# Handing out side steps at every second product of the heads' projections, with other estimates for the delta rule's steps

## The chip, the cores and the metric

The kernel runs on one core of a Trainium2 chip. The metric is the device time of one execution in microseconds (us). Three runs of the kernel before gave 2916.89, 2920.38 and 2922.33 us; their median, 2920.38 us, is the time that the change is measured against.

## What is computed

One inference step of a decoder layer (`DEPTH` is 1, width 2048) for a prompt of 512 tokens and a sample group of 8 sequences with 4 tokens each, all in fp32. Cut to what matters here:

```python
h = rmsnorm(x, norm_mix_g)
sq, sk, sv, gq, gk, gv, ga, gb, gz = split_cols(h @ w_in, IN_SPLITS)
o_sb  = stick_breaking_attention(q, k_all, v_all, ...)      # 8 heads x 128
o_gdn = gated_delta_rule(gdn_q, gdn_k, gdn_v, log_decay, beta, gdn_s0)   # 8 heads x 128
o_gdn = rmsnorm(o_gdn, gdn_out_norm_g) * silu(gz)
x = x + concat(o_sb, o_gdn) @ w_out
x = x + cross_attention(rmsnorm(x), mem_k, mem_v) @ w_xo    # 4 heads, 256 memory tokens
x = x + (silu(gate) * up) @ w_down                          # SwiGLU, hidden 5632
```

The gated delta rule works on chunks of tokens. For each chunk a unit lower triangular matrix (built from k.k, the decays and beta) is inverted, and then a state of 128 x 128 runs through the chunks one after the other: v_new = u - w state, o = q state + qk v_new, state = g state + k v_new.

## The kernel before, in words

**Dense work.** Every projection is made in products. One product (`products`, L212) multiplies one 128x128 block of a weight with 544 columns (512 of the prompt, 32 of the sample) of the activations. Weight and activation are both split into a high and a low part, and three of the four cross terms are computed, in two halves of 272 columns: six matmuls a product. A projection of 128 output columns (`project`, L225) is 16 products. Its weights are loaded from HBM in pieces of 512 KB (`weights`, L195) and split by ScalarE (L206) and VectorE (L207).

**Side work.** What the heads need beside that is written as Python generators: `sb_head` (stick-breaking, prompt), `sb_sample` (the same for the sample, over the paged cache), `gdn_head` (delta rule, prompt), `gdn_sample`. Each runs until its next `yield` and so is cut into steps of some matmuls and what VectorE (DVE), ScalarE (ACT) and GpSimd (POOL) do with their results. A step yields two numbers: an estimate of its length on TensorE (PE) in us, and a delay until its successor may be issued (1.5 when it is left out).

**The planner.** `Side` (L404) interleaves both at build time. It has a clock `now` and a `credit`. After each product `tick(0.68)` (L222, L455) adds 0.68 to the clock and 0.68 x `ratio` to the credit (at most 8), and while the credit is positive it takes a step whose successor delay has passed (`pick`), which adds the step's length to the clock and takes it from the credit. At most `limits` = (2, 1) generators run at a time: two heads, and one sample generator behind them. Before the projections of head n begin, `settle(n)` (L2299) forces the first four steps of head n-2 and whatever is left of head n-3, due or not (`finish`). The order of these calls sets the priority in which the framework's scheduler then arranges the instructions; it can still pass over one that it takes to be not ready. [...]

**The stages around the change** (kern, L2306 to L2359): projections and heads of the eight stick-breaking heads, the gates, projections and heads of the eight delta heads (`side.ratio` 0.65 over both), then eight gate projections (`gate_head`, ratio 2), then `drain`. The output projection, cross attention and the feed-forward part follow; the feed-forward part has an order written out by hand and no planner.

**A delta head's chain** (`gdn_head` L1045, `invert` L906): transposes of q, k, v; the decays (L1067 to L1076: exp on ACT, products on POOL); k.k and k.q (L1080, L1086), whose results DVE multiplies with what POOL made of the decays (L1083, L1088); a 16x16 inversion in small DVE operations through HBM (`invert16`); then two levels (16, 32) of each: four matmuls (L955) and a mask by DVE (L956), four matmuls (L960) and a subtraction by DVE (L962), four transposes (L919) and a copy by ACT (L921); a last level of two half-size products (L941, L946); then for each of four blocks: k.state (L1104) and DVE L1108, the inverse times that (L1111) with DVE L1112 and ACT L1113, and the new state and output (L1116, L1124, L1125) with DVE L1121 and L1127. At the end comes a norm (L1132) and the transposes of the output. The change touches the pairs that the steps from `invert`'s levels on yield.

Of the kernel before, what the change touches and what calls it, by code (L numbers as in the profile page):

```python
# [51 lines left out]
def bc(ap, shape):  # L52
    return ap.broadcast_to(shape)
# [202 lines left out]
class Stats:  # L256


    def __init__(self, c):
        self.c, self.seen = c, set()  # L260
        self.acc = c.tt("acc")
# [142 lines left out]
class Side:  # L404
# [4 lines left out]
    def __init__(self, c):  # L409
        self.c = c  # L410
        self.hi, self.lo, self.on = [], [], [[], []]
        self.now, self.credit, self.ratio, self.limits = 0.0, 0.0, 0.8, (2, 0)

    def put(self, g, low=False, tiles=None):

        e = [g, 0.0, tiles, 0]
        (self.lo if low else self.hi).append(e)
        return e
# [36 lines left out]
    def tick(self, dense):  # L455
        self.now += dense
        if not self.left():
            self.credit = 0.0
            return
        self.credit = min(self.credit + dense * self.ratio, 8.0)  # L460
        while self.credit > 0:
            e = self.pick()
            if e is None:
                break
            self.step(e)
# [402 lines left out]
def invert16(c, gt):  # L868

    nc = c.nc
    gt16 = c.tt("g16")
    g, t, prod = gt16[:32, 0:256], gt16[:32, 256:512], c.tt("p16")[:32]
    src, dst = c.scr[0], c.scr[1 + c.inv % 2]
    c.inv += 1

    def whole(x):
        return x.rearrange("(a x) -> a x", a=4)[:, : P * P].rearrange("a (j i) -> j a i", i=P)

    def blocks(x):
        return x.rearrange("(n x) -> n x", n=32)[:, : 16 * P].rearrange("n (r i) -> n r i", i=P)[:, :, :16]

    gv, tv = (x.rearrange("p (r i) -> p r i", r=16) for x in (g, t))
    nc.gpsimd.tensor_copy(t, c.id16)
    yield 0.0, 1.0
    nc.sync.dma_start(whole(src), v3(gt))
    yield 0.0, 2.5
    nc.sync.dma_start(gv, blocks(src))
    yield 0.0, 2.5  # L890
    nc.gpsimd.tensor_scalar(g, g, -1.0, None, ALU.mult)
    for i in range(1, 16):
        p3 = prod[:, : i * i].rearrange("p (n j) -> p n j", n=i)
        nc.vector.tensor_mul(p3, tv[:, :i, :i].rearrange("p j n -> p n j"), bc(gv[:, :i, i : i + 1].rearrange("p j o -> p o j"), [32, i, i]))
        nc.vector.tensor_reduce(tv[:, i, :i], p3, mybir.AxisListType.X, ALU.add)
        if i % 4 == 3:
            yield 0.0, 1.2 + i / 8
    nc.sync.dma_start(blocks(dst), tv)
    yield 0.0, 2.5
    tr = c.tt("T")  # L900
    nc.sync.dma_start(v3(tr), whole(dst))
    yield 0.0, 8
    return tr


def invert(c, gt, nc_, levels, res):  # L906

    nc = c.nc  # L910
    gv = v3(gt, nc_)

    def wide(m):
        return bc(m.rearrange("p (o i) -> p o i", o=1), [P, nc_, P])

    def transposed(x, n=P):
        ps = c.aux()
        for a in range(nc_):
            nc.tensor.transpose(ps[:n, a * n : (a + 1) * n], x[:n, a * P : a * P + n], c.ident[:n, :n])  # L919
        t = c.tt("TT")  # L920
        nc.scalar.copy(t[:n, : nc_ * n], ps[:n, : nc_ * n])  # L921
        return t

    if levels[0] == 16:
        tr = yield from invert16(c, gt)
        tt = transposed(tr)
    else:
        ps = transposes(c, gt, nc_)
        tr, tt = c.tt("T"), c.tt("TT")
        nc.vector.tensor_mul(v3(tr, nc_), v3(ps, nc_), wide(c.m1))  # L930
        nc.vector.tensor_sub(v3(tr, nc_), wide(c.ident), v3(tr, nc_))
        nc.gpsimd.tensor_mul(v3(tt, nc_), gv, wide(c.m1t))
        nc.gpsimd.tensor_sub(v3(tt, nc_), wide(c.ident), v3(tt, nc_))
    yield 0.12 * nc_
    for s in levels:
        if s == H:
            ttv = v3(tt, nc_)
            x = c.tt("X")
            ps = c.aux()
            for a in range(nc_):  # L940
                nc.tensor.matmul(ps[H:, a * H : (a + 1) * H], gv[:H, a, H:], tr[:H, a * H : (a + 1) * H], start=True, stop=True, tile_position=(0, H))  # L941
            nc.vector.tensor_copy(x[H:, : nc_ * H], ps[H:, : nc_ * H])
            yield 0.11 * nc_, .8
            ps = c.aux()
            for a in range(nc_):
                nc.tensor.matmul(ps[:H, a * H : (a + 1) * H], x[H:, a * H : (a + 1) * H], ttv[H:, a, H:], start=True, stop=True, tile_position=(H, 0))  # L946
            nc.vector.tensor_sub(ttv[:H, :, H:], ttv[:H, :, H:], ps[:H, : nc_ * H].rearrange("p (a i) -> p a i", a=nc_))
            yield 0.11 * nc_, .8
            continue
        trv, ttv = v3(tr, nc_), v3(tt, nc_)  # L950
        x = c.tt("X")
        xv = v3(x, nc_)
        ps = c.aux()
        for a in range(nc_):
            nc.tensor.matmul(ps[:, a * P : (a + 1) * P], gv[:, a, :], trv[:, a], start=True, stop=True)  # L955
        nc.vector.tensor_mul(xv, v3(ps, nc_), wide(c.lev[s]))  # L956
        yield 0.22 * nc_, 1.1
        ps = c.aux()
        for a in range(nc_):
            nc.tensor.matmul(ps[:, a * P : (a + 1) * P], xv[:, a, :], ttv[:, a], start=True, stop=True)  # L960
        second = [ap.rearrange("p c (q b s) -> p c q b s", b=2, s=s)[:, :, :, 1, :] for ap in (ttv, v3(ps, nc_))]
        nc.vector.tensor_sub(second[0], second[0], second[1])  # L962
        yield 0.22 * nc_, 1.7
        if s != levels[-1]:
            n = H if s * 2 == H else P
            tr = transposed(tt, n)
            yield 0.12 * nc_, 1.4
    res.append(tt)


def transposes(c, src, n=4, ps=None):
    ps = c.aux() if ps is None else ps
    for a in range(n):
        c.nc.tensor.transpose(ps[:, a * P : (a + 1) * P], src[:, a * P : (a + 1) * P], c.ident)  # L974
    return ps
# [12 lines left out]
def v3(t, n=4):  # L988
    return t[:, : n * P].rearrange("p (a d) -> p a d", a=n)
# [55 lines left out]
def gdn_head(c, h, qkv):  # L1045
# [17 lines left out]
    def at(x, a):  # L1063
        return x[:, a * 8 + h : a * 8 + h + 1]
# [32 lines left out]
    for a in range(4):  # L1097
        cols = slice(a * P, (a + 1) * P)
        ve = c.tt("ve")
        if st is None:  # L1100
            rr = vv[:, cols]
        else:
            ps = c.aux()
            nc.tensor.matmul(ps[:, :P], k[:, cols], st, start=True, stop=True)  # L1104
            rr = ve[:, 256:384]
            e = ve[:, 512:513]
            nc.vector.tensor_scalar(e, at(c.ecum, a), -1.0, None, ALU.mult)
            nc.vector.scalar_tensor_tensor(rr, ps[:, :P], e, vv[:, cols], ALU.mult, ALU.add)  # L1108
            yield 0.22, 1
        ps = c.aux()  # L1110
        nc.tensor.matmul(ps[:, :P], tt[:, cols], rr, start=True, stop=True)  # L1111
        nc.vector.tensor_scalar(ve[:, P : 2 * P], ps[:, :P], bke[:, a : a + 1], None, ALU.mult)  # L1112
        nc.scalar.activation(ve[:, :P], ps[:, :P], AF.Identity, scale=br[:, a : a + 1])  # L1113
        yield 0.22, 1.6
        pss = c.aux()
        nc.tensor.matmul(pss[:, :P], kn[:, cols], ve[:, P : 2 * P], start=True, stop=True)  # L1116
        new = c.pb.tile([P, P], F32, tag="st", name="st", bufs=3)
        if st is None:
            nc.vector.tensor_copy(new, pss[:, :P])
        else:  # L1120
            nc.vector.scalar_tensor_tensor(new, st, at(c.gend, a), pss[:, :P], ALU.mult, ALU.add)  # L1121
        pso = c.aux()
        if st is not None:
            nc.tensor.matmul(pso[:, :P], qd[:, cols], st, start=True, stop=False)  # L1124
        nc.tensor.matmul(pso[:, :P], dec[:, cols], ve[:, :P], start=st is None, stop=True)  # L1125
        nc.scalar.activation(ve[:, 384:512], pso[:, :P], AF.Square, accum_out=so[:, a : a + 1])
        nc.vector.tensor_copy(on[:, cols], pso[:, :P])  # L1127
        st = new
        yield 0.66, .9
    nc.sync.dma_start(c.o_gs_p[0, 0, h], st)  # L1130
    out_norm(c, f, so, 4)
    nc.vector.tensor_mul(v3(on), v3(on), col(f, 4))  # L1132
# [413 lines left out]
def cross(c, acts, st, x, side):  # L1546
# [2 lines left out]
    outs, heads = [], []  # L1549
    qs = c.pb.tile([P, 4, NS], F32, name="xqs")  # L1550
    ra = [lambda name, dt=dt, tag=tag: c.act.tile([P, T], dt, tag=tag, name=name, bufs=KD) for dt, tag in ((F32, "ah"), (F32R, "al"))]
    side.limits, side.ratio = (2, 1), 1.5
    for h in range(4):
        ps = project(c, c.w_xq, 0, h * P, acts)
        if h == 0:
# [686 lines left out]
def kern(ctx: ExitStack, tc: tile.TileContext, *args, stop=99):  # L2242
# [27 lines left out]
    side = c.side = Side(c)  # L2270
    with tc.tile_pool(name="pb", bufs=1) as pb:
# [31 lines left out]
            if n > 2:  # L2303
                side.finish(heads[n - 3])

        side.limits, side.ratio = (2, 1), 0.65  # L2306
        for h in range(8):
            settle(h)
            if h == 7:
# [35 lines left out]
                else:  # L2345
                    os[8 + h] = z

        side.ratio = 2
        for h in range(8):
            if h == 2:  # L2350
                settle(16)
# [67 lines left out]
```

## Time and profile before

| | us |
|---|---|
| median of three runs | 2920.38 |
| the profiled execution's own time | 2919.49 |
| its span, first to last instruction | 2917.8 |
| stick-breaking heads (from about 67 to 440 of the span) | 373 |
| delta heads (440 to 930) | 490 |
| gate projections (930 to 1083) | 153 |
| output projection to cross attention (1083 to 1560) | 477 |
| feed-forward part (1560 to the end) | 1358 |

The bounds of the stages are read from the evacuations of the projections (L401, L1016, L2228). The profile counts a matmul as busy from its start to its modelled end. One of 272 columns is listed with some 290 ns, but one starts every 125 ns: a PE that is listed as busy can still have lost time, and only the starts show it. PEclk is the clock that TensorE was granted, 1.00 being full speed.

### The profile page before, as it was taken

How to read it: one execution, taken by the hardware profiler on the slowest of the kernel's cores; microseconds unless marked ns; L12 is line 12 of the kernel's file. 1: busy time of each engine (PE TensorE's matmuls, PEld its weight loads, DVE VectorE, ACT ScalarE, POOL GpSimd, SP SyncE). 2: the span in 40 equal slices, each digit the busy share in tenths (PEclk: the TensorE clock that was granted, in tenths of full speed). 3: DMA queues.
4: the chain of work that ended last, by engine and by line, in shares of the span. 5: the costliest groups of instructions: out<-in, count | busy, mean ns of one | idle time of the engine just before them, and what ended most of it. 6: DMA issues, size and time to landing. Idle time of an engine off the chain costs nothing. (4 is left out here: it accounts for less than half of the span.)

```text
span 2917.8 us, 57065 instructions
## 1 busy us (share of the span) xinstructions
PE 2844.4 (97%) x22442; PEld 2726.1 (93%) x22442; DVE 2006.2 (69%) x3168; ACT 1447.2 (50%) x2760; POOL 718.9 (25%) x858
## 2 busy tenths in 40 slices
PE   8999999999999999999999999999999999999998
PEld 7998888888989989999789999999999999999998
DVE  5553434667676554537488888888888887888886
ACT  5445435534445354425654444444444446555675
POOL 3111112213112110003242334334333334221200
PEclk9999999999999999999999999999999999999999
DMA  7335443453342374442444555455455549866653
GB/s 223 99 89 160 141 137 119 125 172 90 91 136 83 109 219 147 146 121 91 160 141 139 160 171 166 149 166 164 149 154 172 153 137 267 264 207 190 195 170 96
DMA packets 632692, 442.71 MB, mean 152 GB/s; under 512 B 36107, under 2 KB 559704, under 8 KB 632424
## 3 DMA queue, kind: packets, MB, share of 16 engines
q1 hardware_dynamic: 600600, 384.64, 44.4%
q0 software_dynamic: 22176, 42.90, 4.7%
q10 hardware_dynamic: 9648, 11.54, 1.1%
q8 instruction: 176, 2.88, 0.4%
q14 instruction: 92, 0.75, 0.1%
HBM read 359.23 MB, written 79.75 MB: 150 GB/s over the span
## 5 line engine op out<-in xcount | busy, mean ns | idle before, releaser
L2044 PE MATMUL gu<-pr,wh 128*128 128x272 f32 x4944 | 673.2, 288 | 6.4 <-ACT pr L1673 2.7
L2044 PEld LDWEIGHTS gu<-pr,wh 128*128 128x128 f32 x4944 | 641.1, 189 | 8.0 <-ACT pr L1673 3.1
L218 PE MATMUL mm<-ah,wh 128*128 128x272 f32 (+1 forms) x2464 | 546.6, 302 | 5.8 <-ACT ah L334 3.5
L218 PE MATMUL mm<-al,wh 128*128 128x272 f32 (+1 forms) x2464 | 524.5, 292 | 0.7 <-DVE al L249 0.7
L218 PE MATMUL mm<-ah,wl 128*128 128x272 f32 (+1 forms) x2464 | 518.0, 291 | 0.1
L1924 PE MATMUL bank<-pr,wh 128*128 128x272 f32 x2464 | 466.1, 289 | 1.0 <-ACT bank L1952 1.0
L218 PEld LDWEIGHTS mm<-ah,wh 128*128 128x128 f32 (+1 forms) x2464 | 389.7, 189 | 33.7 <-issue 20.5
L207 DVE TENSOR_TENSOR wl<-wr,wh 128x512 fp32r<-128x512 f32 (+1 forms) x340 | 243.4, 719 | 230.6 <-ACT wh L206 219.7
L218 PEld LDWEIGHTS mm<-al,wh 128*128 128x128 f32 (+1 forms) x2464 | 391.4, 189 | 3.7 <-DVE al L249 0.9
L218 PEld LDWEIGHTS mm<-ah,wl 128*128 128x128 f32 (+1 forms) x2464 | 388.0, 189 | 2.4 <-issue 0.8
L1924 PEld LDWEIGHTS bank<-pr,wh 128*128 128x128 f32 x2464 | 385.6, 188 | 2.9 <-ACT bank L1952 2.7
L206 ACT CAST wh<-wr 128x512 fp32r<-128x512 f32 (+1 forms) x340 | 208.2, 615 | 314.1 <-PE mm L218 267.2
L2044 PE MATMUL gu<-pr,wl 128*128 128x272 f32 x2472 | 361.8, 289 | 1.9 <-issue 1.8
L1924 PE MATMUL bank<-pr,wl 128*128 128x272 f32 x1232 | 354.1, 287 | 0.0
L2044 PEld LDWEIGHTS gu<-pr,wl 128*128 128x128 f32 x2472 | 330.5, 189 | 2.3 <-issue 1.9
L1822 DVE TENSOR_TENSOR wl<-sum,wh 128x1024 fp32r<-128x1024 f32 x172 | 219.6, 1277 | 76.5 <-ACT wh L1818 76.5
L1924 PEld LDWEIGHTS bank<-pr,wl 128*128 128x128 f32 x1232 | 231.9, 188 | 0.0
L1818 ACT CAST wh<-sum 128x1024 fp32r<-128x1024 f32 x172 | 180.3, 1049 | 77.4 <-PE gu L2044 42.8
L1822 DVE TENSOR_TENSOR wl<-raw,wh 128x1024 fp32r<-128x1024 f32 x133 | 202.9, 1527 | 15.3 <-ACT wh L1818 13.4
L1818 ACT CAST wh<-raw 128x1024 fp32r<-128x1024 f32 x133 | 139.8, 1051 | 102.3 <-PE gu L2044 95.0
L2109 POOL DMA_DIRECT2D pr<-hT x154 | 81.9, 548 | 254.2 <-PE bank L1924 227.7
L1811 DVE TENSOR_TENSOR sum<-raw,sum 128x1024 f32<-128x1024 f32 x86 | 136.0, 1582 | 0.7
(530 smaller groups left out, 4153.0 us busy)
## 6 DMA issues: line engine op xcount, KB each, us to landing
raw<-in_w_gate_up SPq DMA_DIRECT2D x176, 512.0 KB
wr<-in_w_in SPq DMA_DIRECT2D x108, 512.0 KB
raw<-in_w_down SPq DMA_DIRECT2D x176, 256.0 KB
hT<-hs SPq DMA_DIRECT2D x154, 272.0 KB
pr<-hT POOLq DMA_DIRECT2D x154, 272.0 KB, 6.6
page<-in_cache_sb_k SPq DMA_DIRECT2D x128, 128.0 KB
page<-in_cache_sb_v SPq DMA_DIRECT2D x64, 256.0 KB
wr<-in_w_out SPq DMA_DIRECT2D x32, 512.0 KB
```

Source lines behind the costliest of these rows:

```text
L206: nc.scalar.copy(hi[:, :m, :n], raw[:, k : k + m, :n])
L207: nc.vector.tensor_sub(lo[:, :m, :n], raw[:, k : k + m, :n], hi[:, :m, :n].bitcast(F32))
L218: c.nc.tensor.matmul(ps[:n, h, :HT], l[:, :n], r[:, h * HT : (h + 1) * HT], start=first and i == 0, stop=last and i == 2,)
L1811: self.f.c.nc.vector.tensor_sub(self.a[q], self.a[x], self.a[y])
L1818: self.f.c.nc.scalar.copy(self.hi[q], self.left(q))
L1822: self.f.c.nc.vector.tensor_sub(self.lo[q], self.left(q), self.hi[q].bitcast(F32))
L1924: self.c.nc.tensor.matmul(self.c.bank[bank][:, o], t[x][:, s, i * P : (i + 1) * P], pairs[i].op[q][r], start=new and not (i or n), stop=se ...
L2044: self.c.nc.tensor.matmul(bank, w[:, i * P : (i + 1) * P], self.pairs[i].op[q][r], start=start and n == 0, stop=n == 23, skip_group_check= ...
L2109: self.c.nc.gpsimd.dma_start(t, self.hT[2 * g + pair, :, max(0, 2 * n - 1) + k])
```

## The change

The planner can be told to hand out steps only at every second product (`every`), and is told so in the two stages of the heads; the ratio there goes from 0.65 to 0.75. From the gate projections on it is again every product. In the delta rule the estimated lengths go down to about 55% (0.22 to 0.12 for a group, 0.66 to 0.36 for the state step), and the delays become 1.1 to 1.5 where they were 0.8 to 1.7. No instruction is added or taken away.

```diff
@@ class Side, __init__
         self.now, self.credit, self.ratio, self.limits = 0.0, 0.0, 0.8, (2, 0)
+        self.every, self.ticks = 1, 0
@@ class Side, tick
         self.credit = min(self.credit + dense * self.ratio, 8.0)
+
+        self.ticks += 1
+        if self.ticks % self.every:
+            return
         while self.credit > 0:
@@ invert, level 64: L943 and L948
-            yield 0.11 * nc_, .8
+            yield 0.06 * nc_, 1.2
...
-            yield 0.11 * nc_, .8
+            yield 0.06 * nc_, 1.2
@@ invert, levels 16 and 32 (and 2): L957, L963, L967
-        yield 0.22 * nc_, 1.1
+        yield 0.12 * nc_, 1.5
...
-        yield 0.22 * nc_, 1.7
+        yield 0.12 * nc_, 1.5
...
-            yield 0.12 * nc_, 1.4
+            yield 0.12 * nc_, 1.5
@@ gdn_head: L1109, L1114, L1129
-            yield 0.22, 1
+            yield 0.12, 1.2
...
-        yield 0.22, 1.6
+        yield 0.12, 1.5
...
-        yield 0.66, .9
+        yield 0.36, 1.1
@@ cross, L1552
-    side.limits, side.ratio = (2, 1), 1.5
+    side.limits, side.ratio, side.every = (2, 1), 1.5, 1
@@ kern, before the heads, L2306
-        side.limits, side.ratio = (2, 1), 0.65
+        side.limits, side.ratio, side.every = (2, 1), 0.75, 2
@@ kern, before the gate projections, L2348
-        side.ratio = 2
+        side.ratio, side.every = 2, 1
```

## Prediction

> **What bounds the kernel now.** I read the page's first part, then busy time by stage, then the waits of TensorE, then the timeline of the longest waits.
>
> ```profile
> PE 2844.4 (97%) x22442; PEld 2726.1 (93%) x22442; DVE 2006.2 (69%) x3168; ACT 1447.2 (50%) x2760; POOL 718.9 (25%) x858
> ...
> core 0: us, PE busy (x) PEld busy (x) DVE busy (x) ACT busy (x) POOL busy (x), PEclk, DMA share, GB/s
> ...
> 67.00:440.00 373.00, 368.74 (x2897) 329.76 (x2897) 166.10 (x287) 170.44 (x378) 65.95 (x118) 1.00 0.42 126
> 440.00:930.00 490.00, 469.90 (x3748) 427.49 (x3747) 318.04 (x813) 231.50 (x614) 102.59 (x168) 0.98 0.41 118
> 930.00:1083.00 153.00, 146.37 (x1115) 138.16 (x1114) 85.20 (x219) 64.88 (x163) 33.95 (x47) 0.97 0.48 140
> ...
> 67.00:1083.00 1016.00, 985.00 (x7756) 895.41 (x7756) 569.34 (x1318) 466.81 (x1154) 202.49 (x333) 0.98 0.42 124
> ```
>
> PE bounds the kernel: 2844.4 of 2917.8 us. The change only reorders, and only in the three stages from 67 to 1083. There PE is not busy for 1016.0 - 985.0 = 31.0 us (4.3 with the stick-breaking heads, 20.1 with the delta heads, 6.6 in the gate projections), and the granted clock is 0.98 and 0.97 in the last two: 490 x 0.02 + 153 x 0.03 = 14.4 us of full-speed time withheld. Waits and slow clock together, 45 us, bound what an order can give. The order can't make a matmul cheaper:
>
> ```profile
> 799.64 0.38 PE L1116 MATMUL aux<-ve,kn 128*128 128x128 f32 x2
> 799.86 0.39 PE L1124 MATMUL aux<-st,qd 128*128 128x128 f32 x2
> 800.09 0.39 PE L1125 MATMUL aux<-ve,cumrow 128*128 128x128 f32 x2
> 800.23 0.50 PE L218 MATMUL mm<-ah,wh 128*128 128x272 f32 x2
> 800.56 0.41 PE L218 MATMUL mm<-al,wh 128*128 128x272 f32 x2
> 800.81 0.41 PE L218 MATMUL mm<-ah,wl 128*128 128x272 f32 x2
> ```
>
> Columns: start, length, engine and line. Starts are 0.25 us apart for two dense matmuls, so a product takes 0.75 us; they are 0.22 us apart for one side matmul of 128x128 (two records). So the old estimate, 0.22 a matmul, is the true length, and the new one is half of it. The planner's clock will run slow after delta steps; their new delays are therefore longer in truth than they read. From 799.64 to 800.56 six side records and two dense matmuls take 0.92 = 6 x 0.112 + 0.25: going into side work and out of it costs nothing.
>
> ```profile
> PE aux L960 <- DVE X L956: 6.2, 2, 4.5
> PE aux L715 <- ACT kT L704: 4.9, 4, 2.7
> PE aux L715 <- POOL win L686: 4.1, 2, 2.8
> PE aux L919 <- DVE TT L962: 3.9, 2, 3.3
> PE aux L1111 <- DVE ve L1108: 3.1, 3, 1.3
> ...
> DVE gt L1083 <- POOL gt L1082: 15.9, 7, 5.5
> ```
>
> Columns: sum in us, times, longest. Most of the loss lies in few events, and these are side steps that were issued before their operand was there. The longest:
>
> ```profile
> 703.90 0.29 PE L218 MATMUL mm<-ah,wh 128*128 128x272 f32 x1
> 708.73 1.98 PE L960 MATMUL aux<-TT,X 128*128 128x128 f32 x8 [4.54 <-DVE X L956]
> ...
> 706.27 0.69 DVE L1083 TENSOR_TENSOR gt<-gt,aux 128x512 f32<-128x512 f32 x1 [5.45 <-POOL gt L1082]
> 707.38 0.69 DVE L1088 TENSOR_TENSOR cumrow<-cumrow,aux 128x512 f32<-128x512 f32 x1 [0.43 <-POOL cumrow L1087]
> 707.99 0.68 DVE L956 TENSOR_TENSOR X<-aux,lev 128x512 f32<-128x512 f32 x1
> ...
> 708.00:711.00 3.00, 2.27 (x11) 2.28 (x12) 1.53 (x4) 0.00 (x0) 2.61 (x6) 0.64 0.40 95
> 711.00:714.00 3.00, 3.00 (x20) 2.46 (x19) 0.16 (x1) 0.48 (x2) 1.00 (x3) 0.79 0.01 0
> ```
>
> One head's gt product (L1083) stands on DVE waiting for POOL; the other head's mask (L956) is queued behind it, and PE behind that, with every dense product behind PE. After 4.54 us of idleness the clock is 0.64 and 0.79 for 6 us, which costs 3 x 0.36 + 3 x 0.21 = 1.7 us more.
>
> **What the change does to the order.** I worked the planner's bookkeeping through, call by call, with the yields of the code. Before, 12 of the 16 products L960 of the prompt's heads come at most one product (0.75 us) after their L955; after, 3 of 16, the rest two or more. The transposes L919 go the other way: from 1 of 16 at no or one product to 5 of 16 in the same slot as L960 (a long step of another generator carries the clock past the delay). L1111 behind L1104 stays at two products, 21 of 24 before and 20 of 24 after. The page steps of the samples (0.6, delay 0.4) were one product apart in 59 of 80 cases and become two apart in 69. The same number of steps falls into 273 slots where it fell into 338; slots with four steps or more go from 6 to 15. A delay of 1.5 is longer than two products (1.36), so a head that nothing else overtakes waits for four.
>
> **The cost, part by part**, in PE time of these stages.
>
> L956 to L960: 6.2 us in 2 waits. What L960 needs is DVE's 0.68 us plus its queue. One product more covers a plain queue, not the wait for POOL, because the spacing from the decay step to L1083's step is already two or more products in six of eight heads and is exactly two after. I take half: -3.1, and half of the 1.7 us of slow clock: -0.9. Bounds: -7.9 and 0.
>
> L962 to L919: 3.9 us in 2 waits. Five pairs in one slot now need DVE's 0.42 us covered by the other generator's matmuls, 0.9 us and more each (eight records of 0.112). I take +1.0. Bounds: -3.9, and +2.1 (5 x 0.42).
>
> L1108 to L1111, 3.1 us: same spacing, 0. Bounds -3.1 and +3.1.
>
> L715, 5.9 us of the 9.0 in these stages (the rest is in cross attention):
>
> ```profile
> L715 PE MATMUL aux<-kT,win 128*32 128x128 f32 x512 | 28.1, 289 | 5.9 <-POOL win L686 4.1 <-ACT kT L704 1.8
> ```
>
> The row is of 67 to 1083. POOL's 4.1 is the start of a sample, a queue on POOL that a step of distance doesn't clear; the copies by ACT (1.8) get a product more, of which I take -1.3. Bounds: -5.9 and 0.
>
> The states of the first delta sample (L1212):
>
> ```profile
> 749.50 5.14 PE L1212 MATMUL aux<-sqk,s 128*128 128x8 f32 x40
> 754.50 0.57 PE L218 MATMUL mm<-ah,wh 128*128 128x272 f32 x1
> ...
> 754.00:757.00 3.00, 3.00 (x15) 3.00 (x15) 0.00 (x0) 0.62 (x1) 0.00 (x0) 0.50 0.54 162
> 757.00:760.00 3.00, 3.00 (x16) 3.00 (x15) 1.11 (x2) 1.21 (x2) 0.00 (x0) 0.50 0.00 0
> ```
>
> Five steps of 8-column matmuls run in one block though the planner had them a product apart, and the clock stands at 0.50 for the 6 us behind it, 3.0 us lost, though PE was busy throughout. After, they are two to four products apart. I take -2.2, bounds -3.0 and 0.
>
> Settling. Before, head 4's last two steps were forced, three products after its L1125. After, heads 1, 2 and 3 are forced; for 1 and 2 the transposes still come six products after L1125, for head 3 two (1.5 us).
>
> ```profile
> 873.74 0.39 PE L1125 MATMUL aux<-ve,cumrow 128*128 128x128 f32 x2
> ...
> 875.73 0.69 DVE L1132 TENSOR_TENSOR on<-on,sm 128x512 f32<-128x512 f32 x1
> ...
> 983.53 0.39 PE L1125 MATMUL aux<-ve,cumrow 128*128 128x128 f32 x2
> ...
> 986.80 0.69 DVE L1132 TENSOR_TENSOR on<-on,sm 128x512 f32<-128x512 f32 x1
> ```
>
> From L1125 to the end of the norm are 2.7 and 4.0 us, so PE could wait 1.2 to 2.5 us once, less what the scheduler puts in between. I take +1.0, bounds 0 and +2.5.
>
> Fuller slots: nine more with four steps or more. Not shown by a row of its own; nearest is the block above. I take +0.5; from above it is rival A.
>
> The rest of the 31.0 us is 31.0 - 6.2 - 3.9 - 3.1 - 5.9 = 11.9 us, single waits of a microsecond or so of many kinds. All spacings but the zeros grow from one or two products to two: I take a sixth, -2.0. A new order also draws new collisions: bounds -6 and +6.
>
> Nothing is late at the end:
>
> ```profile
> L1136 ACT ACTIVATE o<-aux,gains x8: 669/688/689, 625.0 to 1044.3; 128x512 f32<-128x512 f32 x8
> L401 DVE TENSOR_TENSOR gz<-mm,rstd x8: 712/724/725, 955.8 to 1081.9; 128x544 f32<-128x544 f32 x8
> ```
>
> The last head's output (L1136) starts 37.6 us before the last gate projection is evacuated. By the bookkeeping the last side step moves from product 884 to 895 of 912, 8 us later; the cover of three gate projections shrinks to one, and costs nothing while it is there. No DMA is moved past a dense weight load except the pages and states, on SP's queue with the weights; their rate over a stage is unchanged.
>
> Sum: -3.1 - 0.9 + 1.0 - 1.3 - 2.2 + 1.0 + 0.5 - 2.0 = -7.0 us. The profiled execution took 2919.49 us, 0.9 below the median of the three: 2919.5 - 7.0 = 2912.5 us.
>
> **Rivals.**
>
> A, slower: the clock gate decides. Slots of four and more steps put matmuls with few rows or columns side by side, and the rows at 754 show that the clock falls behind such a block with no idleness at all, by 3.0 us each time. If four of the nine new full slots do that and the sum's gains halve (-3.5), the kernel is 12 - 3.5 = 8.5 us slower: 2928. It decides from two such blocks on. For it: the rows at 754. Against it: most full slots hold 128x128 matmuls of heads, and the run of six at 799.64 left the next dense pair at 0.25 us. [...]
>
> B, no difference: the scheduler passes over what it takes to be unready, so the planner's distance matters little, and what remains (DVE behind POOL at L1083, 15.9 us in 7 waits, up to 5.5) depends on engines that the change doesn't touch. Then only the redrawing of the 12 us is left, within 5: 2919.5, or 2915 to 2924. For it: the spacing of the decay step to L1083's is hardly changed. Against it: L960's is.
>
> C, faster by more: PE saves at the borders of side runs, of which there are 338 - 273 = 65 fewer. The second dense pair behind a side run starts 0.33 us after the first, 0.08 more than in a stream; were that a cost, 65 x 0.08 = 5.2 us more would go: 2907. Against it is the sum 0.92 above: the first pair starts early by as much. [...]
>
> **How the numbers follow.** The forecast has 0.45, A 0.17, B 0.30, C 0.08. The predicted time is 2912.5. The bounds of the forecast's terms, taken together as independent, reach about 7 to 8 us to either side: 2905 to 2920. The range takes in C and most of A: 2900 to 2928. About 0.2% (5.8 us) is what a measurement of this kernel can tell from no change. Faster by more than that: C and a good part of the forecast, and a little of B: 0.50. Within it: the rest of the forecast and most of B: 0.33. Slower: A: 0.17.
>
> **What would show it.** Right: PE's idle time from 67 to about 1075 falls below 27 us and PEclk of the delta stage is 0.99; the row L960 <- X L956 falls by half; L1212 no longer stands in one block of 40. Wrong in a step: a wait of L919 or of the output's transposes above 2 us; PEclk of 0.97 or less with the delta heads (A); rows of L1083 and L956 with the same long waits (B). Work moved past 1083, or a changed time of the feed-forward part, would make the whole account wrong.

## The result, and the profile after

The changed kernel takes 2891.46 us (median of four runs, 2891.30 to 2892.98), the kernel before, beside it, 2920.18 us (2916.89 to 2922.33). The ratio is 0.9902 [0.9888, 0.9916]: 28.7 us faster. 2912.5 was predicted, and 2900 to 2928 as the range: the sign was right, the size a quarter of what came. The profiled execution took 2891.30 us, its span is 2889.6.

Lines behind L464 carry a number 5 higher in the changed kernel (L956 is L961, L960 L965, L1082 L1087, L1083 L1088, L1212 L1217). The first part of its page, busy time by engine:

```profile
PE 2821.6 (98%) x22442; PEld 2713.2 (94%) x22442; DVE 2015.0 (70%) x3168; ACT 1446.6 (50%) x2760; POOL 728.8 (25%) x858
```

Its busy time by stage; the rows are the stick-breaking heads, the delta heads, the gate projections, and the three together:

```profile
core 0: us, PE busy (x) PEld busy (x) DVE busy (x) ACT busy (x) POOL busy (x), PEclk, DMA share, GB/s
53.00:435.00 382.00, 377.80 (x2980) 340.81 (x2980) 168.08 (x296) 171.63 (x381) 70.14 (x120) 1.00 0.42 125
435.00:908.00 473.00, 457.77 (x3749) 421.11 (x3749) 321.56 (x808) 230.61 (x609) 107.65 (x168) 0.99 0.42 123
908.00:1050.00 142.00, 139.80 (x1123) 133.88 (x1122) 90.59 (x224) 66.36 (x168) 35.23 (x47) 1.00 0.52 152
53.00:1050.00 997.00, 975.37 (x7847) 895.80 (x7848) 580.24 (x1327) 468.59 (x1157) 213.02 (x335) 1.00 0.44 128
```

The delta heads are 17 us shorter, the gates 11, the stick-breaking heads, whose own pairs are unchanged, 4. PE's idle time over the three is 997.0 - 975.4 = 21.6 us where it was 31.0, and the clock is 0.99 and 1.00 where it was 0.98 and 0.97. TensorE's waits, and DVE's wait for POOL, of the changed kernel (sum in us, times, longest):

```profile
PE aux L720 <- ACT kT L709: 5.2, 4, 2.7
PE aux L1116 <- DVE ve L1113: 3.7, 5, 1.5
PE aux L924 <- DVE TT L967: 2.7, 2, 1.9
PE aux L924 <- DMA T<-scr: 2.6, 1, 2.6
...
PE aux L965 <- DVE X L961: 1.0, 2, 0.8
...
DVE gt L1088 <- POOL gt L1087: 10.0, 6, 2.2
```

L965 waits 1.0 us where it waited 6.2. The row of L720 (L715) for POOL's win, 4.1 us before, is gone altogether. DVE's longest wait for POOL has gone from 5.5 to 2.2 us.

**One account for all kernels.** To compare the kernels I take the three stages together, from the evacuation of the first projections to that of the last gate projection, and split their time in three: PE's idle time as listed; the time in which the trace has the granted clock at about half, which costs up to half of its length (two dense matmuls start 0.45 us apart at 880 us of the changed kernel, at half clock, and 0.25 us apart at 885, at full clock); and the rest. Before: 1027.7 = 31.3 idle + 30.7 / 2 + 981.0. After: 996.7 = 21.8 + 6.8 / 2 + 971.5. So of the 31.0 us that the stages lost, 9.5 are idle time, 12.0 clock, and 9.5 appear in neither: over that time PE is listed as busy, and no run here shows where it went. Ahead of the stages 1.2 us go as well, and behind them, where nothing was changed, 4.1 come back (1835.8 to 1839.9): 28.1 us, against 28.2 between the two profiled executions. That unchanged code takes 1834.7 to 1839.2 us in fifteen of the sixteen other kernels and 1843.0 in q1, so the 4.1 are about the spread of single executions.

| kernel | steps at every n-th product | median us | ratio to before | three stages | idle | half clock | rest |
|---|---|---|---|---|---|---|---|
| before | 1 | 2920.2 | | 1027.7 | 31.3 | 30.7 | 981.0 |
| after | 2 | 2891.5 | .9902 [.9888, .9916] | 996.7 | 21.8 | 6.8 | 971.5 |
| e1: slots and ratio | 2 | 2887.5 | .9892 [.9872, .9911] | 995.8 | 18.9 | 3.4 | 975.2 |
| e2: estimates | 1 | 2903.5 | .9945 [.9927, .9963] | 1008.2 | 26.2 | 6.8 | 978.6 |
| e3: ratio | 1 | 2908.9 | .9962 [.9948, .9975] | 1016.0 | 28.1 | 20.4 | 977.7 |
| e4: after, old ratio | 2 | 2890.4 | .9897 [.9875, .9919] | 997.4 | 16.3 | 6.8 | 977.7 |
| m1: least delay | 1 | 2903.1 | .9930 [.9906, .9955] | 1010.7 | 28.1 | 13.6 | 975.8 |
| m2: delays | 1 | 2908.1 | .9953 [.9936, .9971] | 1016.9 | 32.0 | 17.0 | 976.4 |
| m3: lengths | 1 | 2902.1 | .9934 [.9906, .9962] | 1010.7 | 25.3 | 13.7 | 978.6 |
| m4: e1, every third | 3 | 2904.0 | .9934 [.9910, .9958] | 1008.6 | 22.8 | 20.5 | 975.6 |
| p1: before, POOL early | 1 | 2895.2 | .9914 [.9897, .9930] | 1002.4 | 20.1 | 6.8 | 978.9 |
| p2: after, POOL early | 2 | 2889.1 | .9887 [.9870, .9903] | 1001.7 | 20.2 | 17.1 | 973.0 |
| q1: before, sample later | 1 | 2899.7 | .9936 [.9916, .9955] | 1001.1 | 22.1 | 0 | 979.0 |
| q2: after, sample back | 2 | 2890.2 | .9903 [.9876, .9930] | 997.0 | 22.3 | 3.4 | 973.0 |
| r1: ratio 0.70 | 1 | 2904.8 | .9947 [.9927, .9967] | 1012.8 | 28.1 | 20.5 | 974.5 |
| s1: e1, sample later | 2 | 2893.7 | .9913 [.9896, .9931] | 998.0 | 20.8 | 3.4 | 975.5 |
| s3: e2, sample later | 1 | 2904.9 | .9953 [.9936, .9971] | 1009.5 | 24.8 | 10.2 | 979.6 |
| s4: p2, states apart | 2 | 2889.3 | .9892 [.9875, .9908] | 997.6 | 21.8 | 6.8 | 972.4 |

The medians are of two to five runs (before: seven to ten beside each group), which lie within 7 us of each other, but for q1 (9 us) and q2 (14 us, three runs at 2887 to 2890 and one at 2901). The last four columns are of one execution. The rest hardly moves (971 to 981), while idle time plus half of the half-clock time goes from 19.7 to 46.7: what these orders change is mostly waits and clock.

### The profile page after: what moved, and what is told of

Its sections match the earlier page's. It is cut to its first block, busy times and chain, and to the rows that moved or that the text cites. A ratio compares the mean times of both kernels' runs of the same rounds, so it can differ in the third digit from the quotient of the medians.

```text
span 2889.6 us, 57077 instructions
## 1 busy us (share of the span) xinstructions
PE 2821.6 (98%) x22442; PEld 2713.2 (94%) x22442; DVE 2015.0 (70%) x3168; ACT 1446.6 (50%) x2760; POOL 728.8 (25%) x858
## 5 line engine op out<-in xcount | busy, mean ns | idle before, releaser
L1827 DVE TENSOR_TENSOR wl<-raw,wh 128x1024 fp32r<-128x1024 f32 x133 | 203.5, 1531 | 15.2 <-ACT wh L1823 13.7
```

What stands on the lines that cost most here:

```text
L1827: self.f.c.nc.vector.tensor_sub(self.lo[q], self.left(q), self.hi[q].bitcast(F32))
```

## The experiments

The theories in the expectations are: D, the distance of two products clears waits; E, the new estimates do; L, luck, that is, any new order would do about as well; B, steps handed out in pairs save PE time at the borders of side runs; P, a collision on POOL's queue makes the long waits.

**Which part does it.** Four kernels: the old pairs with every second product and ratio 0.75 (e1); the new pairs alone (e2); the ratio alone (e3); the whole change with the old ratio (e4).

```diff
e2  -  side.limits, side.ratio, side.every = (2, 1), 0.75, 2
    +  side.limits, side.ratio, side.every = (2, 1), 0.65, 1
e3  -  side.limits, side.ratio = (2, 1), 0.65
    +  side.limits, side.ratio = (2, 1), 0.75
e4  -  side.limits, side.ratio, side.every = (2, 1), 0.75, 2
    +  side.limits, side.ratio, side.every = (2, 1), 0.65, 2
```

> The old lengths and delays of the delta rule, handed out at every second product with ratio 0.75. Theory D (distance: two products between the steps of a chain, and with it fewer waits and fewer spells of half clock, which comes from handing out at every second product): most of the gain of the heads' stages, 2898 to 2904 us, the delta stage near 473 us, the gate stage (every product in both kernels) still near 152 us. Theory E (the new lengths and delays do it): within 5 us of 2920. Theory L (luck: any other order draws its collisions anew, and the kernel before had drawn badly): anything from 2890 to 2925, with no relation between stage and edit.

> The new lengths and delays alone, every product, ratio 0.65. Theory D: 2908 to 2915 us, the delta stage within 6 us of before (489), only the gate stage near 142 us. Theory E: 2895 us or less. Theory L: anything from 2890 to 2925.

> Ratio 0.75 alone, all else as before. Theories D and E: 2917 to 2925 us, since neither distance nor estimates change; half clock in the heads' stages as long as before (some 30 us). Theory L: off 2920 by more than 6 us in either direction.

> The changed kernel with the ratio back at 0.65. Theories D and E: 2888 to 2897 us, as the ratio only sets how soon work is handed out. Theory L: 2890 to 2920, by chance near neither.

Measured: 2887.5, 2903.5, 2908.9 and 2890.4 us. e1 is 10 us below the range of theory D, e2 lies between those of D and E, and e3, for which both expected no change, is 11 us faster, as only L allowed; e4 came as D and E expected. Handing out at every second product, with the new ratio, gives the whole gain without the new estimates, and somewhat more than the whole change, though the two intervals overlap. The estimates alone give 16.6 us, the ratio alone 11.3; on top of the slots (the steps at every second product) each is about nothing. The slots with the old ratio and the old estimates were not run. The parts don't add up: they remove in part the same losses, or, as L has it, any of them only leaves an unlucky order. The estimates alone leave the long wait where it was. From the timeline of e2, one row of DVE and one of PE (start, length, engine, line, idle time before):

```profile
705.58 0.69 DVE L1088 TENSOR_TENSOR gt<-gt,aux 128x512 f32<-128x512 f32 x1 [3.93 <-POOL gt L1087]
...
707.98 0.63 PE L924 MATMUL aux<-ident,TT 64*64 64x64 f32 x4 [3.61 <-DVE TT L967]
```

And the busy time of e2 in the two stretches of 3 us there (columns as in the stages above, the granted clock third from the end):

```profile
706.00:709.00 3.00, 1.02 (x6) 0.85 (x7) 1.29 (x3) 0.35 (x1) 2.73 (x7) 0.61 0.31 87
709.00:712.00 3.00, 3.00 (x17) 2.63 (x17) 0.85 (x3) 0.63 (x2) 0.77 (x2) 0.50 0.12 11
```

Another instruction of PE is hit (L924 in place of L965), at the same place and after the same wait of DVE for POOL, and the clock falls behind it. So it isn't the pair L961 to L965 that is too close.

**Distance, lengths and delays apart.** m1 keeps the old pairs and makes every delay in the heads' stages at least two products (1.36); m2 takes only the new delays, m3 only the new lengths; m4 is e1 with every third product.

```diff
m1  -  e[1] = self.now + lat
    +  e[1] = self.now + max(lat, self.least)  
m4  -  side.limits, side.ratio, side.every = (2, 1), 0.75, 2
    +  side.limits, side.ratio, side.every = (2, 1), 0.75, 3
```

> The kernel before with every delay in the two head stages raised to at least 1.36 (two products), handed out at every product still, ratio 0.65; the gate projections as before. Theory D (the distance between a step and its successor is what counts): the delta stage near 470 us as with handing out at every second product, in all 2895 to 2904 us. Theory B (it is the handing out in pairs, with fewer borders between dense and side work): delta stage 480 us or more, 2908 to 2920 us. Theory L (luck): no telling, 2890 to 2925.

> The kernel before with the new delays and the old lengths, every product, ratio 0.65. Theory D: the delays carry the gain of the estimates (2903.5 us with both), 2900 to 2908 us, the gate stage near 142 us. If it is the lengths: 2915 to 2922 us and the gate stage near 152 us. Theory L: no telling.

> The kernel before with the new lengths and the old delays, every product, ratio 0.65. Theory D: since the clock runs slower the old delays are longer in truth, by at most 0.4 us a step; a part of the gain at most, 2910 to 2920 us, the gate stage 148 to 153 us. If it is the lengths: 2900 to 2906 us. Theory L: no telling.

> Old lengths and delays, ratio 0.75, handed out at every third product (2887.5 us with every second). Theory D: waits fall on, but heads no longer end in time and settling forces whole rows of steps without products between them; more forced steps, delta stage 466 to 485 us, 2887 to 2907 us. Theory B: as good or better than every second, 2880 to 2889 us.

Measured: 2903.1, 2908.1, 2902.1 and 2904.0 us. m1 and m4 lie in D's ranges and outside B's, though m1's delta stage takes 476 us and not 470; m3 came as the lengths would have it, and m2 lies a hair above D's range. A row of DVE's timeline in m1 (its lines behind L413 are 1 higher):

```profile
710.69 0.69 DVE L1084 TENSOR_TENSOR gt<-gt,aux 128x512 f32<-128x512 f32 x1 [4.77 <-POOL gt L1083]
```

And the longest of TensorE's waits in m1 (sum, times, longest):

```profile
PE aux L1105 <- DVE st L1120: 6.8, 2, 4.7
```

Distance alone doesn't clear the long wait: with every delay at two products or more, DVE still stands 4.77 us behind POOL, and PE 4.7. Nor does it clear the other wait for POOL. The row of L715 for POOL's win, 4.1 us in 2 waits in before, e2, e3, m2, m3, p1, q1 and s3 (4.2 in r1), has no entry in m1, nor in any kernel that hands out at every second or third product. But in m1 the same line waits 5.0 us for ACT's copies of kT instead, against 5.9 for both engines in before. At every second product it is 2.0 to 3.7 us for ACT, and 3.1 at every third: there the wait does get shorter. More distance is not better: against before beside it, every third product gains 18.8 us and every second 32.7. With the new lengths the gate projections get shorter (143 us in m3, 150 in m2, 152 before), but the lengths are not needed for it: r1 and p1, with the old ones, have 142.5.

**What stands ahead on POOL's queue.** The prediction shows PE and DVE at the longest wait of before; the matmuls whose result L956 masks (L955 at 701.25) were over by 702.31, and DVE ran it at 707.99, behind L1083. POOL's timeline ahead of it (start, length, engine, line):

```profile
701.58 0.46 POOL L1165 TENSOR_TENSOR sqk<-sqk,sctmp 128x128 f32<-128x128 f32 x1
702.12 0.42 POOL L1163 TENSOR_TENSOR sctmp<-raws,convw 128x128 f32<-128x128 f32 x1
702.50 1.29 POOL L1069 TENSOR_TENSOR qd<-qd,cv 128x512 f32<-128x512 f32 x1
703.75 0.46 POOL L1165 TENSOR_TENSOR sqk<-sqk,sctmp 128x128 f32<-128x128 f32 x1
704.28 0.42 POOL L1163 TENSOR_TENSOR sctmp<-raws,convw 128x128 f32<-128x128 f32 x1
704.78 0.45 POOL L1165 TENSOR_TENSOR sqk<-sqk,sctmp 128x128 f32<-128x128 f32 x1
705.19 1.04 POOL L1082 TENSOR_TENSOR gt<-cumrow,sm 128x512 f32<-128x512 f32 x1
```

And the busy time of before around both of its long waits (the fifth busy column is POOL):

```profile
696.00:708.00 12.00, 8.19 (x70) 7.96 (x68) 6.08 (x14) 3.49 (x10) 11.37 (x19) 1.00 0.17 46
936.00:953.00 17.00, 12.94 (x107) 12.20 (x105) 9.81 (x18) 6.63 (x29) 14.39 (x23) 1.00 0.16 47
```

POOL is busy for 11.37 of 12 us and 14.39 of 17 us. The small operations are the convolution of a delta sample (`gdn_sample` L1161 to L1166), whose first three steps put 12 multiplications and 9 additions on POOL; the head's decay products (L1069, L1082) stand among them. By the planner's bookkeeping, sample 1 hands these steps out at products 593, 598 and 602, the head in question at 598 and 600; sample 2 at 785, 790 and 793, another head at 791 and 792. With every second product the stick-breaking sample ahead of it ends later, and sample 1 begins at 610 or later, behind the head. POOL in the changed kernel:

```profile
685.55 1.27 POOL L1074 TENSOR_TENSOR qd<-qd,cv 128x512 f32<-128x512 f32 x1 [3.41 <-issue]
689.57 1.04 POOL L1087 TENSOR_TENSOR gt<-cumrow,sm 128x512 f32<-128x512 f32 x1 [2.75 <-ACT cumrow L1081]
690.69 1.04 POOL L1092 TENSOR_TENSOR cumrow<-cumrow,sm 128x512 f32<-128x512 f32 x1
...
699.83 0.96 POOL L1168 TENSOR_TENSOR sqk<-raws,convw 128x128 f32<-128x128 f32 x1
```

The head's products come first, 10 us ahead of the sample's, and POOL even waits before them.

p1 takes the collision out of before in another way, by issuing both decay products a step earlier with a delay of 6; p2 does the same to the changed kernel.

```diff
     nc.scalar.activation(dec[:, :NP], dec[:, :NP], AF.Exp)
-    yield 0.9
+    gt = c.tt("gt")
+    nc.gpsimd.tensor_mul(v3(gt), v3(dec), col(br2, 4))
+    nc.gpsimd.tensor_mul(v3(dec), v3(dec), col(rk, 4))
+    yield 0.9, 6.0
```

> The kernel before, with the two POOL products of a delta head's decays moved from the step of k.k and k.q into the step before it, and that step's delay raised to 6, so that DVE needn't wait for POOL; nothing else. Theory P (the two longest waits are POOL's queue: the first steps of a delta sample put some 24 POOL operations ahead of a head's decay products, DVE stands behind them, PE behind DVE, and the clock falls behind PE's idleness; the edits that helped had moved the samples' start away from that): the waits near 704 and 949 us and the half clock behind them go, 2902 to 2910 us. Theory D (distance of the steps as such): within 5 us of 2920, since no distance in the levels changes. Theory L: no telling.

> The changed kernel with the POOL products moved as in the edit of the kernel before. Theory P: one collision is left to remove (a wait of 1.9 us near 877 us and 6.8 us of half clock behind it), 2884 to 2889 us. Theory D: 2889 to 2893 us. Theory L: no telling.

p1 takes 2895.2 us, 26 below the kernel before beside it, with steps handed out at every product; both long waits are gone. That is 7 us less than theory P had expected, and more than the collision's own price: in before its two waits of PE (4.5 and 3.3 us) and the half clock behind them (3.4 and 6.8 us, half of which is lost) come to 13.0 us. The rest of p1's gain came with the new order and is not explained by the collision. p2 takes 2889.1 us, 2.4 below the changed kernel, within the runs' spread, at the border of P's range and D's. The two ways of removing the collision don't add up either.

**Moving the sample.** q1 is before with an empty step of 22 us ahead of the sample's convolution; q2 the changed kernel with the sample let in again beside the stick-breaking sample; r1 before with a ratio of 0.70, for which the bookkeeping gives both collisions, as in before.

```diff
q1  +    yield 0.0, 22.0                  # first line of gdn_sample
q2  +    side.limits = (2, 2)             # before side.put(gdn_sample(...))
r1  -  side.limits, side.ratio = (2, 1), 0.65
    +  side.limits, side.ratio = (2, 1), 0.70
```

> The kernel before, with an empty first step of delay 22 put ahead of the delta samples, so that their POOL operations come behind the decays of heads 3 and 7 by the planner's bookkeeping (products 613 and 804 against 598 to 600 and 796 to 798); nothing else. Theory P: both long waits and the half clock behind them go, 2900 to 2909 us. Theory D: 2917 to 2923 us. Theory L: no telling.

> The changed kernel with two sample generators allowed at a time from the fourth delta head on, which puts the first delta sample's start back from product 612 to 594, on top of head 3's decays (600 to 602), as in the kernel before. Theory P: a wait of 3 to 5 us near 690 us and a spell of half clock behind it come back, 2896 to 2903 us. Theory D: 2888 to 2894 us. Theory L: no telling.

> The kernel before with ratio 0.70, a change that means nothing. By the bookkeeping the samples' starts (products 593 to 604 and 785 to 794) lie on the decays of heads 3 (599 to 600) and 7 (792 to 794). Theory P: both long waits stay, near 704 and 945 us, each above 2 us with half clock behind it; 2905 to 2922 us. Theory L: as likely without them as with them, and below 2900 us as likely as above.

DVE's waits for POOL in q1:

```profile
DVE gt L1083 <- POOL gt L1082: 8.9, 7, 1.9
```

The same in q2, and the wait of PE that comes of it:

```profile
DVE gt L1088 <- POOL gt L1087: 13.5, 7, 3.6
PE aux L924 <- DVE gt L1088: 2.7, 1, 2.7
```

And the busy time of q2 around that wait:

```profile
690.00:693.00 3.00, 0.52 (x5) 0.30 (x3) 0.54 (x1) 0.00 (x0) 2.77 (x5) 1.00 0.00 0
693.00:696.40 3.40, 3.20 (x18) 2.00 (x18) 1.51 (x3) 0.98 (x2) 3.09 (x7) 0.52 0.29 82
```

With the sample later DVE's waits fall to those of the changed kernel, and q1 takes 2899.7 us, 21.4 less than before beside it (its stages would give 26.6; it pays 6 us in new waits as the output projection begins). With the sample back the collision is back: POOL is busy for 2.77 of 3 us, PE for 0.52, and half clock follows. That the sample's work on POOL makes the long wait is shown in both directions. Its price is not: q2's median is 2890.2 us, not the 2896 to 2903 expected, into which one of its four runs falls. In the profiled run the collision cost about 2.7 + 1.7 us, and other waits and spells fell by as much. r1 is a miss of theory P: it expected both waits, each above 2 us, and 2905 to 2922 us. r1 takes 2904.8 us, PE's wait of 3.6 us at 710 is there, and near 945 none is. In its DVE timeline:

```profile
940.93 0.69 DVE L1083 TENSOR_TENSOR gt<-gt,aux 128x512 f32<-128x512 f32 x1 [1.34 <-POOL gt L1082]
```

Here the head's product stands at 939.9 us among the sample's operations (925.2 to 945.5) as it did in before, and DVE waits 1.34 us where it waited 3.09. So standing in that queue isn't enough. POOL had been idle twice ahead of it (1.5 us at 932, 1.2 us at 936), which suggests that it counts how densely the queue is filled; the bookkeeping doesn't tell this.

**Does the collision explain what is left?** s1 and s3 put q1's empty step into e1 and e2; s4 is p2 with a delay of 4 behind each of the sample's state steps.

```diff
s4  -            yield 0.9
    +            yield 0.9, 4.0           # gdn_sample, after each sequence's L1217 matmuls
```

> Every second product with ratio 0.75 and the old estimates (2887.5 us), with the empty step of delay 22 ahead of the delta samples. Theory P alone (all that counts is that the sample's POOL operations miss the heads' decays): as the edit at every product, 2896 to 2902 us, or as 2887.5 where nothing is left to miss. Theory P with D (distance takes a further 8 to 12 us of waits, in this and the stick-breaking stage): 2883 to 2890 us. Theory L: no telling.

> The new lengths and delays at every product, ratio 0.65 (2903.5 us, with one collision left near 706 us), with the empty step ahead of the delta samples. Theory P: the collision and its half clock go, and the estimates add nothing beyond: 2893 to 2900 us. Theory E (the estimates gain by themselves): 2885 to 2892 us. Theory L: no telling.

> The changed kernel with POOL's products early (2889.1 us, 13.6 us at half clock near 769 us behind two steps of 8-column matmuls within 3 us, with 0.7 us of idleness before them), and the delay of those steps raised from 1.5 to 4. If the steps of 8-column matmuls lower the clock by lying close together: no half clock there, 2881 to 2885 us. If it is the idleness: half clock stays, 2887 to 2891 us.

Measured: 2893.7, 2904.9 and 2889.3 us. s1 lies between the ranges of P alone and of P with D, and some 6 us above e1, which has no empty step. s3 missed by every account: without the collision (DVE's longest wait for POOL's decay product is 1.9 us) the estimates alone were no faster than with it. s4 removed the spell of half clock that it was made to remove (the delta heads take 473 us, p2's 478), but two others, 3.4 us each, came up at 851 and 937 us, and the time stayed where it would have been expected with the spell.

Over all of them: the nine edited kernels that hand out at every product take 2895 to 2909 us, every one of them less than before; the seven that hand out at every second product take 2887 to 2894. Before is the slowest of eighteen orders of the same work. So a good part of the gain is that its order was an unlucky one: the six in which nothing was done on purpose about the collision on POOL (e2, e3, m1, m2, m3, r1) take 2905 us on average, 11 to 21 less than before beside them, and in e3 and r1 only the ratio was moved. How many of the long waits an order has goes with its time: e3 and m2, where DVE waits 3.9 us or more for POOL at both places, take 2908 to 2909 us, the other four, where one such wait is left or (m3) none above 2.2 us, 2902 to 2905. Before has both and takes 2920, so these waits are not all that it suffers from. Another 15 us go with the slots (2890 on average of the seven). How much of these is the collision that the slots avoid as well, and how much distance, is not separated: p1 and q1, which avoid it, reach 2895 and 2900 without slots, but s3 doesn't. e1 is the fastest version measured, 4 us below the changed kernel, with intervals that overlap.

## Why the prediction was wrong

**The frame held in the main.** The prediction said that an order can only give back waits and withheld clock in the three stages, 45 us at most, and these two fell from 46.7 to 25.2 us. But 9.5 us, a third of what the stages lost, were in neither, and for them the frame had no place. PE's idle time fell below 27 us, the clock of the delta heads rose to 0.99, the row of L960 behind L956 fell by more than half, all as listed under "right". The sum took 7.0 us, in which idle time counts -4.4 and clock, with the full slots, -2.6. Measured: -9.5 and -12.0, and -9.5 in neither. So of the 21 us by which the forecast fell short, the clock makes 9.4, the part in neither 9.5 and idle time 5.1; what happened outside the stages (-1.2 and +4.1) takes 2.9 off. The sign owes something to luck: each of the seventeen edited orders is faster than before.

**The step that failed, L956 to L960.** The sum took half of that wait and of the clock behind it, "because the spacing from the decay step to L1083's step is already two or more products in six of eight heads", so that DVE's wait for POOL would stay. It looked at the distance inside the head. The wait came from whose work was ahead on POOL's queue, and the change moved that: the sample began behind the head. The row went from 6.2 to 1.0 us, -5.2 where -3.1 was taken, and DVE's wait from 15.9 to 10.0. As a reading of the mechanism this is the main error; in time it is only some 2 us and the clock behind them. Rival B rested on the same sentence and fell with it.

**L715.** POOL's 4.1 us were to stay and 1.3 of ACT's 1.8 to go. The reverse came: in these stages POOL's part is 0 and ACT's 2.1, so that the row fell by 3.8 us where 1.3 was taken. Longer delays alone don't do this: m1 has 5.0 us there, all behind ACT.

**The clock** is the term that was mis-sized most, -2.6 us where -12.0 came: two of its spells were priced, 0.9 and 2.2 us, and their bounds held 4.7 of the 14.4 us of withheld time that the prediction had counted. The other spells stood in no term. The trace of before has six spells, 30.7 us at half clock, behind waits of 2.8, 4.5 and 3.3 us, behind the block of L1212, and twice behind the 32-row matmuls of L1265. One is left, 6.8 us long, behind the 1.9 us wait of L924 at 877. Even with all 14.4 us taken off, the sum would give 2900.7 us, at the lower end of the range and 9 us above the measured time. The bounds of the terms, taken together as the prediction says, reach 9 to 10 us and not 7 to 8; that wouldn't have held the time either.

**L1212** went as forecast. The changed kernel:

```profile
758.83 1.06 PE L1217 MATMUL aux<-sqk,s 128*128 128x8 f32 x8
762.03 1.06 PE L1217 MATMUL aux<-sqk,s 128*128 128x8 f32 x8
766.26 0.95 PE L1217 MATMUL aux<-sqk,s 128*128 128x8 f32 x8
769.33 0.96 PE L1217 MATMUL aux<-sqk,s 128*128 128x8 f32 x8
```

The steps stand 3 to 4 us apart, and no half clock follows.

**Right in kind and small:** L919, +1.0, has 2.7 us behind DVE and 2.6 behind a DMA where it had 3.9 (+1.4); that is the wait above 2 us that was listed as wrong for a step, and it didn't decide. L1111 went from 3.1 to 3.7 (0 forecast). The settling's +1.0 did not come: no wait of the output's transposes for L1132's result is left. Rival A didn't occur in this kernel, though in p1 and p2 6.8 and 13.6 us at half clock came behind steps of 8-column matmuls. The 4.1 us behind the stages were listed as a sign that would make the account wrong (a changed time of the feed-forward part, which is 2.0 of them); they stand in code that both kernels share and are about the spread over the other kernels.

**Open.** The rest column is 974.0 us on average for every second product and 978.0 for every product, before included. Fewer borders of side runs (rival C, 5.2 us) would make such a difference, and so would waits that the list doesn't show. No run tells the two apart, and the 9.5 us of the changed kernel stay open with them.

## What to carry to other kernels

Where a wait ends with another engine, open that engine's own timeline and ask whose instructions stand ahead in its queue: distance within one generator says nothing of a second generator on the same engine. Clock that the profile shows as withheld belongs into the bounds as a term of its own: here 30.7 us at half clock became 6.8 us while idle time went from 31.3 to 21.8 us. One kernel against another doesn't measure an idea about order when a changed ratio alone is worth 11 to 16 us (e3, r1): try several small changes of order beside the one that is meant, and see whether it stands out from them.

## What the runs showed of the hardware

In p1 the granted clock fell to 0.51 while PE was listed as busy. From its PE timeline:

```profile
734.22 0.96 PE L1212 MATMUL aux<-sqk,s 128*128 128x8 f32 x8
735.03 0.50 PE L218 MATMUL mm<-ah,wl 128*128 128x272 f32 x2
735.37 0.95 PE L1212 MATMUL aux<-sqk,s 128*128 128x8 f32 x8
...
737.01 0.95 PE L1212 MATMUL aux<-sqk,s 128*128 128x8 f32 x8
737.82 0.80 PE L218 MATMUL mm<-ah,wh 128*128 128x272 f32 x2
```

The busy time of p1 in the two stretches that follow:

```profile
737.80:741.20 3.40, 3.40 (x17) 3.40 (x17) 0.00 (x0) 0.00 (x0) 0.00 (x0) 0.51 0.59 164
741.20:744.60 3.40, 3.40 (x18) 3.40 (x17) 0.00 (x0) 1.27 (x2) 0.00 (x0) 0.50 0.41 132
```

PE waits for nothing in the 3.4 us ahead of 737.8, but three steps of eight 8-column matmuls take about 2.2 us of them (starts of what follows taken as ends); then the clock is at half for 6.8 us. The same in p2, before its fall of the clock and behind it:

```profile
755.00:769.00 14.00, 13.19 (x110) 12.55 (x109) 9.65 (x20) 6.00 (x10) 5.52 (x10) 1.00 0.29 78
769.00:772.40 3.40, 3.40 (x20) 3.03 (x19) 0.30 (x1) 0.16 (x1) 0.00 (x0) 0.51 0.82 235
...
779.20:782.60 3.40, 3.40 (x17) 3.40 (x17) 0.20 (x1) 0.00 (x0) 0.00 (x0) 0.50 0.26 77
```

With 0.8 us of idleness in 14 us, 13.6 us at half clock follow; with the state steps set apart (s4) there are none at this place. In the other direction 1.9 us of waiting (L924 at 877.1) came ahead of the 6.8 us spell at 877.9 of the changed kernel. In the three stages of before three spells last 3.4 us and three 6.8 us. By p1's rows PE need not have been idle when the clock fell. That the 8-column steps lower it by lying close together is the author's reading of these rows and of s4, not shown.
